# A fixed order on three engines and a ring of five 128x1024 split buffers in an expert stage, with a scatter that leaves out rows without a token

## The chip, the cores and the metric

The kernel runs on one core of a Trainium2 chip. The metric is device time in microseconds (us) for one execution, as the median of several runs. A core has five engines that run side by side and meet through semaphores: PE multiplies matrices (PEld is its weight load), DVE (vector) and ACT (scalar) work elementwise, POOL here mostly issues indirect DMAs, and SP issues plain DMAs. Sixteen DMA engines move the data.

## The reference

The function is one encoder layer: a token mixer (attention and pooling), then a mixture of 32 experts. Only the second half is touched by the change. Each of 1024 tokens goes to two of 32 experts, 2048 places in all, or 64 on average for each expert.

```python
def run_block(args):
    xs, e = args
    gate, up = jnp.split(xs @ w_gate_up[e], 2, axis=-1)
    return (jax.nn.silu(gate) * up) @ w_down[e]
...
out = jax.ops.segment_sum(yb.astype(jnp.float32) * row_w[:, None], row_tok, num_segments=T + 1)
```

An expert multiplies its tokens (rows of 1024 numbers) by a 1024x1024 matrix, whose two halves are gate and up, and the product of silu(gate) and up (512 numbers) by a 512x1024 matrix. The result, weighted, is added to the token's row. Then follows a layer norm over the rows.

## The kernel before, in words

The stages before the experts (projections, attention, output projection, first layer norm, routing) end at about 935 us. The last of them writes the normed rows to `X1` and their scaled copies to `Y` in HBM, and finds for each expert up to 96 rows (`CAP`) of tokens and weights in `first`. What more than 96 tokens an expert has is done in a loop at the end (`overflow`), whose count `count()` works out.

**Precision.** Every product is made of three: a number is split into a high part of reduced width and the remainder (`split`: ACT casts the high part, DVE subtracts to get the low one), and `mm3` adds high x high, high x low and low x high (L165, L166, L167).

**One expert.** `gather` (POOL) fetches its 96 rows into `xg`, four experts ahead. PE transposes them (`X <- xg`, eight 128x96 pieces in two PSUM tiles), and `split` turns these into `xT`, high and low; there is one `xT` buffer. `gu_half` makes `g` with 24 matmuls and `u` with another 24. `hidden` makes `h` from them (`silu` on ACT, the product with `u` on DVE). PE transposes `h` (`X <- h`, four pieces), `split` makes `hT`, and `down` makes two halves `dn` with 12 matmuls each, which ACT weights into `y`. A scatter on POOL then adds `y` to the rows of `Y`. The code is skewed: `down` of expert e-1 is written after the two products of expert e.

**Weights.** An expert has six pieces of 1 MiB (`we`, 128x2048, c = 0 to 5), in a ring of 18 buffers: 15 of the pool `S` and three of the tag `M`. SP issues a load when the buffer's old piece has been split. `weights_` splits a quarter of a piece (128x512, one k of four) into one of five buffers `wh` just before three matmuls use it.

**Order.** Within each engine the scheduler of the framework orders the instructions by its own costs; the set `MOE_ENG` of engines whose order is that of the code is empty. SP's loads keep the order of the program.

**Rows without a token.** An expert's list has 96 entries; those without a token point to row 1024 or above: for the gather past its bound, so that nothing is moved for them, for the scatter to spare rows behind the 1024 real rows of `Y` (96 for each of four groups of experts, cleared by a load of `zero` during attention), so that all 96 rows are added somewhere.

Of the kernel before, what the change touches and what calls it, by code (L numbers as in the profile page):

```python
# [44 lines left out]
NM = 3  # L45
M_AT = (13, 16, 17)
PRE = 5
MOE_ENG = ()
# [5 lines left out]
COUNT_AT = 1  # L54
# [47 lines left out]
def table():  # L102

    t = np.zeros((NE, NBLK, CAP, 4), np.float32)
    t[..., 0] = 4 * T
    t[..., 1] = T + np.arange(NE)[:, None, None] // 8 * CAP + np.arange(CAP)
    return t.reshape(NE * ROWS, 4)


def body(tc, ctx, A, out):  # L110
# [77 lines left out]
    Y = dr.tile([T + 4 * CAP, D], F32, name="Y")  # L188
# [325 lines left out]
    q = SP.dma_start(Y[T:], A["zero"])  # L514
    tc.keep_in_program_order(q)
# [6 lines left out]
    spare = cp.tile([128, 4, 8], F32, name="spare")[:CAP]  # L522
    POOL.iota(spare, pattern=[[CAP, 4], [0, 8]], base=T + 1, channel_multiplier=1, allow_small_or_imprecise_dtypes=True)
# [490 lines left out]
    idx = rt([3, NE], "idx", I32, 1)  # L1014
    tok, wgt = first[:, 0], first[:, 1]

    def rows_at(c, pad):

        no = rt([NE], "no", F32, 3)
        if isinstance(pad, bass.AP) and pad.shape[1] == NE:  # L1020
            DVE.scalar_tensor_tensor(no, tok, 0.0, pad, op0=OP.is_equal, op1=OP.mult)
        else:
            DVE.tensor_scalar(no, tok, 0.0, pad, op0=OP.is_equal, op1=OP.mult)
        DVE.scalar_tensor_tensor(idx[:, c], tok, -1.0, no, op0=OP.add, op1=OP.add)


    rows_at(2, pay[:CAP, 0, 0, 3:4])
# [5 lines left out]
    def transposed(src, n, name, t=None):  # L1033

        t = t or turn_to(n, name)
        for g in range(0, n, 4):
            p = pt([4, CAP], "X", 3)
            for k in range(4):
                PE.transpose(p[:, k], src[:, (g + k) * 128:(g + k) * 128 + 128], ident[:CAP, :CAP])  # L1039
            split(t[:, 0, g:g + 4], t[:, 1, g:g + 4], p)  # L1040
        return t
# [17 lines left out]
    split_ = {}  # L1059

    def weights_(e, c, g):

        if (e, c, g) in split_:
            return split_[e, c, g]
        ahead(stream.index((e, c)) + 1)
        h = split_[e, c, g] = mt([2, 512], "wh", F32R, WH_BUFS)
        split(h[:, 0], h[:, 1], pieces[e, c][:, g])
        return h

    def product(ps, x, e, c, k0):  # L1070

        for g in range(4):
            h, k = weights_(e, c, g), k0 + g
            mm3(ps, (x[:, 0, k], x[:, 1, k]), (h[:, 0], h[:, 1]), k == 0, k == (3 if c >= 4 else 7))
# [306 lines left out]
```

## Time and profile before

| | us |
|---|---|
| median of three runs | 1589.37 (1589.34 to 1590.09) |
| the profiled execution's own time | 1583.73 |
| its span, first to last instruction | 1581.9 |
| experts' stage: first gu matmul to the start of the last dn matmul | 945.80 to 1535.71 |
| granted TensorE clock over the span | 0.978 |

The profile is of one execution, which was 5.6 us shorter than the median of the runs. An engine's busy time in it is the union of its instructions; a matmul's shown length (0.39) holds its way through the array, and the next one starts 0.23 after it.

### The profile page before, as it was taken

What the parts mean: (1) busy time and instruction counts of PE and PEld (TensorE: products, weight loads), DVE (VectorE), ACT (ScalarE), POOL (GpSimd) and SP (SyncE); (2) the same over time, 40 slices, a digit from 0 to 9 for tenths busy, and PEclk for the clock granted to TensorE, in tenths of its full rate; (3) what the DMA queues carried; (4) which work ended last, traced back from release to release, by engine and by line L of the source; (5) the groups of instructions that cost most, each with busy time, mean ns of one, the idle gap of its engine ahead of it and who ended that gap; (6) DMA issues with size and microseconds to landing.
All of it is one profiled execution on the core that took longest, in us unless ns stands there. A gap on an engine that the chain in (4) does not pass through costs nothing.

```text
span 1581.9 us, 23148 instructions
## 1 busy us (share of the span) xinstructions
PE 1504.2 (95%) x7627; PEld 1188.8 (75%) x7627; DVE 1219.3 (77%) x2670; ACT 989.0 (63%) x1955; POOL 336.4 (21%) x232
## 2 busy tenths in 40 slices
PE   8999999999999999999999969999999999999970
PEld 6988888898898898888887856666666666666640
DVE  5774125988988986675567779899999899999867
ACT  4423124676676676674331128888888888888874
POOL 0001000210211210100004440344444444440010
PEclk9999999999999999999999969999999999999995
DMA  7156224855755864427475588999999999999725
GB/s 234 62 175 197 73 80 134 231 191 164 220 190 139 242 193 138 121 97 281 186 283 196 178 290 302 371 381 384 382 385 373 375 380 382 384 380 374 252 31 213
DMA packets 117034, 381.29 MB, mean 241 GB/s; under 512 B 12759, under 2 KB 43863, under 8 KB 91520
## 3 DMA queue, kind: packets, MB, share of 16 engines
q1 hardware_dynamic: 76176, 304.83, 51.5%
q0 software_dynamic: 40160, 74.14, 18.2%
q8 instruction: 61, 1.00, 0.3%
q10 hardware_dynamic: 576, 0.83, 0.2%
q14 instruction: 61, 0.50, 0.1%
HBM read 314.01 MB, written 71.35 MB: 244 GB/s over the span
## 4 chain that ended last, share of the span: by engine, by line
PE 84%; issue 7%; DVE 5%; DMA 2%; ACT 1%; POOL 1%; DVEq 0%; POOLq 0%; SPq 0%; ACTq 0%
PE gu L167 6%; PE gu L166 6%; PE gu L165 6%; PE ps L577 4%; PE pg L165 4%; PE pg L166 4%; PE pg L167 4%; PE po L628 3%; PE dn L166 3%; PE dn L167 3%; PE dn L165 3%; PE X L1039 2%; PE pv L165 2%; PE tp L613 2%; PE pv L167 2%
## 5 line engine op out<-in xcount | busy, mean ns | idle before, releaser
L151 DVE TENSOR_TENSOR wh<-we,wh 128x512 fp32r<-128x512 f32 x768 | 473.0, 683 | 13.6 <-ACT wh L150 10.4
L150 ACT CAST wh<-we 128x512 fp32r<-128x512 f32 x768 | 433.9, 621 | 24.8 <-PE gu L167 6.5
L1083 POOL DMA_INDIRECT xg<-X,idx x32 | 159.9, 4998 | 277.1 <-PE X L1039 266.9
L167 PE MATMUL gu<-wh,xT 128*96 128x512 f32 x512 | 202.8, 396 | 0.0
L165 PE MATMUL gu<-wh,xT 128*96 128x512 f32 x512 | 202.2, 395 | 0.5 <-ACT xT L150 0.5
L166 PE MATMUL gu<-wh,xT 128*96 128x512 f32 x512 | 202.1, 395 | 0.0
L151 DVE TENSOR_TENSOR w<-wraw,w 128x512 fp32r<-128x512 f32 x111 | 75.8, 687 | 92.6 <-ACT w L150 92.2
L150 ACT CAST w<-wraw 128x512 fp32r<-128x512 f32 x111 | 68.5, 621 | 117.7 <-PE pg L167 38.5
L580 ACT ACTIVATE P<-ps,stat 128x256 f32<-128x256 f32 (+7 forms) x128 | 94.8, 741 | 54.7 <-DVE stat L579 53.8
L166 PEld LDWEIGHTS gu<-wh,xT 128*96 128x96 f32 x512 | 83.1, 162 | 36.4
L165 PEld LDWEIGHTS gu<-wh,xT 128*96 128x96 f32 x512 | 83.0, 162 | 36.1 <-ACT xT L150 0.5
L167 PEld LDWEIGHTS gu<-wh,xT 128*96 128x96 f32 x512 | 83.0, 162 | 36.0 <-DVE xT L151 0.5
L166 PE MATMUL dn<-wh,hT 128*96 128x512 f32 x256 | 103.3, 404 | 1.6 <-DVE wh L151 1.5
L165 PE MATMUL dn<-wh,hT 128*96 128x512 f32 x256 | 100.8, 394 | 1.7 <-ACT wh L150 1.7
L167 PE MATMUL dn<-wh,hT 128*96 128x512 f32 x256 | 100.8, 394 | 0.0
L165 PE MATMUL pg<-xT,w 128*128 128x512 f32 x256 | 100.5, 392 | 0.0
L166 PE MATMUL pg<-xT,w 128*128 128x512 f32 x256 | 99.9, 390 | 0.0
L167 PE MATMUL pg<-xT,w 128*128 128x512 f32 x256 | 99.8, 390 | 0.0
L577 PE MATMUL ps<-K,Q 128*128 128x512 f32 (+2 forms) x384 | 98.8, 364 | 0.8 <-DVE z L464 0.8
L579 DVE TENSOR_REDUCE stat<-ps 128x1 f32<-128x256 f32 (+7 forms) x128 | 95.6, 748 | 1.1
L165 PE MATMUL pv<-w,xT 128*128 128x256 f32 x256 | 72.8, 284 | 0.0
L577 PEld LDWEIGHTS ps<-K,Q 128*128 128x128 f32 x384 | 64.7, 189 | 10.7 <-DVE z L464 1.3
(279 smaller groups left out, 3397.3 us busy)
## 6 DMA issues: line engine op xcount, KB each, us to landing
we<-in_we_dram SPq DMA_DIRECT2D x192, 1024.0 KB, 13.6
wraw<-in_w_dram SPq DMA_DIRECT2D x61, 512.0 KB, 3.8
Q<-RQ POOLq DMA_DIRECT2D x64, 256.0 KB, 5.1
RQ<-rh SPq DMA_DIRECT2D x32, 256.0 KB, 3.4
K<-RK POOLq DMA_DIRECT2D x16, 512.0 KB, 4.2
V<-RV POOLq DMA_DIRECT2D x16, 512.0 KB, 5.7
OT<-ohl SPq DMA_DIRECT2D x48, 128.0 KB, 2.3
oT<-OT POOLq DMA_DIRECT2D x6, 1024.0 KB, 10.5
```

Source lines behind the costliest of these rows:

```text
L150: ACT.copy(hi, src)
L151: DVE.tensor_sub(lo, src, r(hi))
L165: PE.matmul(ps, a[0], b[0], start=start, stop=False)
L166: PE.matmul(ps, a[0], b[1], start=False, stop=False)
L167: PE.matmul(ps, a[1], b[0], start=False, stop=stop)
L577: PE.matmul(ps[:, c:c + n], q[:, o, m, qc], Kt[h, m][:, c:c + n], start=o == 0, stop=o == 1)
L579: DVE.tensor_reduce(st_[:, m:m + 1], ps[:, :W], AX.X, OP.max, negate=True)
L580: ACT.activation(Pt[h, i][m][:, :W], ps[:, :W], AF.Exp, bias=st_[:, m:m + 1], accum_out=st_[:, 2 + m:3 + m])
L613: PE.transpose(ps[:, k], p[:, (4 * g + k) * 128:(4 * g + k) * 128 + 128], ident)
L628: PE.matmul(o[:, 0, c], Vt[h][:, a, kt], aT[kt // 4][:, kt % 4, b, c], start=j == 0, stop=j == len(parts) - 1)
L1039: PE.transpose(p[:, k], src[:, (g + k) * 128:(g + k) * 128 + 128], ident[:CAP, :CAP])
L1083: q = POOL.indirect_dma_start(out=x, out_offset=None, in_=X1, in_offset=IO(ap=idx[:, 2 * (e < NXG), expert[e]:expert[e] + 1], axis=0), bou ...
```

## The change

It has three parts.

1. **A fixed order.** PE, ACT and DVE run the experts' stage in the order of the code (`manual_schedule`), and the code is rewritten for that. `product` counts the halves of pieces that PE has used (`state["used"]`); after each one it issues the split of the half that is five ahead (`split_next`), and then whatever was put there to be done (`put(n, ...)`: after n more halves). So the transposes of `h` stand after `g`, those of `xg` after `u`, and the casts, `silu`, the product `h*u`, the weighting `y` and the scatter stand one to three halves behind the matmuls that they need.
2. **Wider splits.** A split is of 128x1024 (two k, six matmuls), in a ring of five such buffers. The ring of pieces is 16 instead of 18 (`NM` 1 for 3).
3. **No spare rows.** The scatter's index of an entry without a token lies past its bound and is left out, as the gather's is; the spare rows, their clearing, and the index list for them are gone. The overflow loop's buffers come from the pool `S`.

```diff
-NM = 3
-M_AT = (13, 16, 17)
-PRE = 5
-MOE_ENG = ()
+NM = 1
+M_AT = (13,)
...
-    Y = dr.tile([T + 4 * CAP, D], F32, name="Y")
+    Y = dr.tile([T, D], F32, name="Y")
...
-    q = SP.dma_start(Y[T:], A["zero"])
...
+    parts = [(e, c, g) for e, c in stream for g in range(2)]
...
+    def split_next():
+        if state["split"] < len(parts):
+            e, c, g = parts[state["split"]]
+            state["split"] += 1
+            ahead(stream.index((e, c)) + 1)
+            h = mt([2, 2, 512], "wh", F32R, WH_BUFS)
+            split(h[:, 0], h[:, 1], pieces[e, c][:, 2 * g:2 * g + 2])
+            ring.append(h)
...
+    def product(ps, x, c, k0):
+
+        for g in range(2):
+            h = ring.popleft()
+            for i in range(2):
+                k = k0 + 2 * g + i
+                mm3(ps, (x[:, 0, k], x[:, 1, k]), (h[:, 0, i], h[:, 1, i]), k == 0, k == (3 if c >= 4 else 7))
+            state["used"] += 1
+            split_next()
+            for f in todo.pop(state["used"], ()):
+                f()
...
-                                    bounds_check=T + 4 * CAP - 1, oob_is_err=True, compute_op=OP.add)
...
+                                    bounds_check=T - 1, oob_is_err=False, compute_op=OP.add)
...
+    with tc.manual_schedule(engines={mybir.EngineType.PE, mybir.EngineType.Activation, mybir.EngineType.DVE}):
...
+        for _ in range(WH_BUFS):
+            split_next()
+        for g, p in enumerate(transposes(gx.pop(0), 8)):
+            taken(x, g, p)
...
+            g = gu_half(x, 0)
+            if e:
+                hT = turn_to(4, "hT")
+                put(1, taken, hT, 0, transposes(h, 4)[0])
+            put(2, ACT.activation, h, g, AF.Silu)
+            u = gu_half(x, 2)
             if e + 1 < NE:
-                x = transposed(gx.pop(e + 1), 8, "xT")
+                x = turn_to(8, "xT")
+                for i, p in enumerate(transposes(gx.pop(e + 1), 8)):
+                    if e:
+                        put(1 + i, taken, x, i, p)
+                    else:
+                        taken(x, i, p)
+            put(3 if 0 < e < NE - 1 else 1, DVE.tensor_mul, h, h, u)
             if e:
                 down(e - 1, hT)
+        hT = turn_to(4, "hT")
+        taken(hT, 0, transposes(h, 4)[0])
+        down(NE - 1, hT)
```

Three places show what this does to the order. On PE, in the middle of the experts' stage, this is where `down` of one expert begins, with the transposes of `h` and of the next `xg` (`X`):

```order
L165 MATMUL dn_11066<-wh_11075,hT_10987 96x512
L1039 MATMUL X_11182<-cst,h_9634 128x96 x4
L1039 MATMUL X_11245<-cst,xg_9574 128x96 x4
L1039 MATMUL X_11252<-cst,xg_9574 128x96 x4
L166 MATMUL dn_11066<-wh_11075,hT_10987 96x512
L167 MATMUL dn_11066<-wh_11075,hT_10987 96x512
```

Before, all twelve transposes stand in one block, after the fourth matmul of `dn`, between the first and the second of three matmuls of one k. With the change the four of `h` stand between `g` and `u`, five halves of pieces later than the product that makes `h`:

```order
L164 MATMUL gu_10707<-wh_10688,xT_10644 96x512
L1029 MATMUL X_10753<-cst,h_9630 128x96 x4
L162 MATMUL gu_10758<-wh_10701,xT_10644 96x512
L163 MATMUL gu_10758<-wh_10701,xT_10644 96x512
L164 MATMUL gu_10758<-wh_10701,xT_10644 96x512
```

The eight of `xg` stand behind `u`, ahead of `dn`. On DVE, at the same place, these rows before are the product `h` and what stands around it:

```order
L151 TENSOR_TENSOR wh_10681<-we_10679,wh_10681 128x512
L1096 TENSOR_TENSOR h_9634<-h_9634,gu_10607 96x512
L151 TENSOR_TENSOR xT_10662<-X_10663,xT_10662 128x384
L151 TENSOR_TENSOR xT_10662<-X_10670,xT_10662 128x384
L151 TENSOR_TENSOR wh_10687<-we_10679,wh_10687 128x512
L151 TENSOR_TENSOR wh_10693<-we_10679,wh_10693 128x512
```

And these with the change:

```order
L148 TENSOR_TENSOR wh_10347<-we_10323,wh_10347 128x1024
L148 TENSOR_TENSOR xT_10328<-X_10329,xT_10328 128x384
L148 TENSOR_TENSOR wh_10360<-we_10358,wh_10360 128x1024
L148 TENSOR_TENSOR xT_10328<-X_10334,xT_10328 128x384
L148 TENSOR_TENSOR wh_10372<-we_10358,wh_10372 128x1024
L1080 TENSOR_TENSOR h_9630<-h_9630,gu_10284 96x512
```

The three jobs that stood together now stand one behind each split. On PE at the stage's start, before, the first expert's eight transposes and four of the second expert's stand ahead of the first product:

```order
L1039 MATMUL X_9660<-cst,xg_9573 128x96 x4
L1039 MATMUL X_9667<-cst,xg_9573 128x96 x4
L1039 MATMUL X_9763<-cst,xg_9574 128x96 x4
L165 MATMUL gu_9677<-wh_9645,xT_9633 96x512
L166 MATMUL gu_9677<-wh_9645,xT_9633 96x512
```

With the change only the first expert's eight do:

```order
L898 MATMUL pr_9453<-ohr_9534 96x64 x2
L1029 MATMUL X_9652<-cst,xg_9570 128x96 x4
L1029 MATMUL X_9657<-cst,xg_9570 128x96 x4
L162 MATMUL gu_9669<-wh_9637,xT_9629 96x512
L163 MATMUL gu_9669<-wh_9637,xT_9629 96x512
```

The second expert's transposes of `xg` all stand behind the first expert's `u`.

## Rows read from the trace of the kernel before

**Rows 1.** The page: the span and the engines' busy time.
```profile
span 1581.9 us, 23148 instructions
PE 1504.2 (95%) x7627; PEld 1188.8 (75%) x7627; DVE 1219.3 (77%) x2670; ACT 989.0 (63%) x1955; POOL 336.4 (21%) x232
```

**Rows 2.** A stretch: length; busy PE, PEld, DVE, ACT, POOL; clock, DMA share, GB/s.
```profile
1000.00:1100.00 100.00, 100.00 (x458) 69.03 (x457) 91.26 (x152) 88.42 (x163) 40.04 (x11) 1.00 1.02 377
```

**Rows 3.** Instructions in order of time, one expert's transposes: start, us, what [idle before].
```profile
1100.21 0.86 ACT L150 CAST xT<-X 128x384 fp32r<-128x384 f32 x2 [1.47 <-PE gu L167]
...
1100.82 1.01 DVE L151 TENSOR_TENSOR xT<-X,xT 128x384 fp32r<-128x384 f32 x2
...
1100.95 0.55 PE L1039 MATMUL X<-cst,h 96*128 96x96 f32 x4
...
1101.47 1.03 PE L1039 MATMUL X<-cst,xg 96*128 96x96 f32 x8
1101.75 1.88 DVE L151 TENSOR_TENSOR wh<-we,wh 128x512 fp32r<-128x512 f32 x3
1102.48 0.16 PEld L166 LDWEIGHTS dn<-wh,hT 128*96 128x96 f32 x1 [0.17 <-DVE wh L151]
...
1102.79 0.40 PE L167 MATMUL dn<-wh,hT 128*96 128x512 f32 x1
```

**Rows 4.** PE in order of time: six transposes of an early expert.
```profile
974.63 0.49 PE L1039 MATMUL X<-cst,h 96*128 96x96 f32 x4
974.96 0.33 PE L1039 MATMUL X<-cst,xg 96*128 96x96 f32 x2
...
975.36 0.39 PE L167 MATMUL dn<-wh,hT 128*96 128x512 f32 x1
```

**Rows 5.** PE: first gu matmuls of experts 3, 9, 31; first dn matmul behind 9's.
```profile
997.35 0.39 PE L165 MATMUL gu<-wh,xT 128*96 128x512 f32 x1
...
1107.19 0.39 PE L165 MATMUL gu<-wh,xT 128*96 128x512 f32 x1
...
1118.31 0.39 PE L165 MATMUL dn<-wh,hT 128*96 128x512 f32 x1
...
1509.98 0.39 PE L165 MATMUL gu<-wh,xT 128*96 128x512 f32 x1
```

**Rows 6.** Splits by shape: count, busy us, mean ns of one, idle time before them.
```profile
L151 DVE TENSOR_TENSOR wh<-we,wh 128x512 fp32r<-128x512 f32 x763 | 469.7, 683 | 12.6 <-ACT wh L150 9.4 <-DMA we<-in_we_dram 1.7
L150 ACT CAST wh<-we 128x512 fp32r<-128x512 f32 x763 | 431.1, 621 | 20.9 <-PE gu L167 6.5 <-PE dn L167 2.6
...
L151 DVE TENSOR_TENSOR xT<-xr,xT 128x1024 fp32r<-128x1024 f32 x8 | 9.8, 1225 | 6.2 <-ACT xT L150 6.2
L150 ACT CAST xT<-xr 128x1024 fp32r<-128x1024 f32 x8 | 8.4, 1051 | 12.0 <-DMA xr<-in_xT_dram 12.0
```

**Rows 7.** PE at the stage's start, in order of time, and the clock there.
```profile
940.81 1.54 PE L1039 MATMUL X<-cst,xg 96*128 96x96 f32 x8 [5.99 <-DMA xg<-X,idx]
945.19 0.90 PE L1039 MATMUL X<-cst,xg 96*128 96x96 f32 x4 [2.84 <-DMA xg<-X,idx]
945.80 0.72 PE L165 MATMUL gu<-wh,xT 128*96 128x512 f32 x1
...
959.67 0.47 PE L165 MATMUL gu<-wh,xT 128*96 128x512 f32 x1 [0.46 <-ACT xT L150]
...
945.80:949.30 3.50, 3.50 (x10) 2.31 (x10) 0.69 (x1) 1.22 (x2) 1.90 (x2) 0.50 0.84 167
```

**Rows 8.** PE at the stage's end, in order of time.
```profile
1529.19 0.47 PE L165 MATMUL dn<-wh,hT 128*96 128x512 f32 x1 [1.66 <-ACT wh L150]
...
1535.71 0.39 PE L167 MATMUL dn<-wh,hT 128*96 128x512 f32 x1
```

**Rows 9.** Loads of weights in 1000 to 1100 and 1360 to 1460: us to landing.
```profile
we<-in_we_dram SPq DMA_DIRECT2D x33, 1024.0 KB, 11.9
...
we<-in_we_dram SPq DMA_DIRECT2D x34, 1024.0 KB, 17.1
```

More of the change, by code (lines that the diff above doesn't have):

```diff
@@ L1019, in rows_at @@
         no = rt([NE], "no", F32, 3)
[L1020 to L1023, printed above, removed]
+        DVE.tensor_scalar(no, tok, 0.0, pad, op0=OP.is_equal, op1=OP.mult)
         DVE.scalar_tensor_tensor(idx[:, c], tok, -1.0, no, op0=OP.add, op1=OP.add)
-    rows_at(2, pay[:CAP, 0, 0, 3:4])
+    rows_at(1, pay[:CAP, 0, 0, 3:4])
     xgs = [rt([D], f"xg{i}", F32, 1) for i in range(NXG)]
@@ L1057, in ahead, with put @@
             pieces[e, c] = w
[L1059 to L1074, printed above, removed]
+    parts = [(e, c, g) for e, c in stream for g in range(2)]
+    ring = deque()
+    todo = {}
+    def split_next():
[6 more added lines that the diff above has]
+            ring.append(h)
+    def put(n, f, *a):
+        todo.setdefault(state["used"] + n, []).append(partial(f, *a))
+    def product(ps, x, c, k0):
[8 more added lines that the diff above has]
+                f()
     ahead(13)
@@ L1086, in gather, with gu_half, scatter, weighted @@
         return x
-    def gu_half(e, x, c):
+    def gu_half(x, c):
         ps = pt([512], "gu", 3, CAP)
-        product(ps, x, e, c, 0)
-        product(ps, x, e, c + 1, 4)
-        return ps
-    def hidden(h, g, u):
-        ACT.activation(h, g, AF.Silu)
-        DVE.tensor_mul(h, h, u)
-        return h
+        product(ps, x, c, 0)
+        product(ps, x, c + 1, 4)
+        return ps
+    def scatter(e, y):
+        q = POOL.indirect_dma_start(out=Y, out_offset=IO(ap=idx[:, 0, expert[e]:expert[e] + 1], axis=0), in_=y, in_offset=None,
+                                    bounds_check=T - 1, oob_is_err=False, compute_op=OP.add)
+        for i, o in enumerate(ysc):
+            if i % 4 != e % 4:
+                tc.declare_no_dep(q.ins, o.ins, reason="another group's rows of Y")
+        ysc.append(q)
+    def weighted(e, y, n, d):
+        ACT.activation(y[:, n * 512:n * 512 + 512], d, AF.Copy, scale=wgt[:, expert[e]:expert[e] + 1])
+        if n:
+            scatter(e, y)
     def down(e, hT):
@@ L1102, in down @@
             d = pt([512], "dn", 2, CAP)
-            product(d, hT, e, 4 + n, 0)
-            ACT.activation(y[:, n * 512:n * 512 + 512], d, AF.Copy, scale=wgt[:, expert[e]:expert[e] + 1])
-        q = POOL.indirect_dma_start(out=Y, out_offset=IO(ap=idx[:, 1, expert[e]:expert[e] + 1], axis=0), in_=y, in_offset=None,
-                                    bounds_check=T + 4 * CAP - 1, oob_is_err=True, compute_op=OP.add)
-        for i, o in enumerate(ysc):
-            if i % 4 != e % 4:
-                tc.declare_no_dep(q.ins, o.ins, reason="another group's rows of Y")
-        ysc.append(q)
+            product(d, hT, 4 + n, 0)
+            put(1, weighted, e, y, n, d)
     def count():
-        pc = pt([2 + 2 * NE + 1], "X", 3)
+        pc = pt([512], "gu", 3)[:, :2 + 2 * NE + 1]
+        ov, ovi = mt([NE], "ov", F32, 1)[:1], mt([2 * NE + 1], "ovi", I32, 1)[:1]
         v, b = mt([3], "cv", F32, 1)[:NE], mt([2 * NE + 1], "cb", BF, 1)[:NE]
@@ L1133, in count @@
         DVE.tensor_scalar(ovi[:, NE:2 * NE], ov, 1.0, float(CAP), op0=OP.add, op1=OP.mult)
-        return ovi
+        yield ovi
     def overflow(x, ovi):
```

62 lines of the change are left out of this document (29 added, 33 removed).

## The prediction

> **What bounds the kernel now.** I read the page first: PE is busy for 95% of the span [rows 1], so a change pays only where PE waits, works slowly, or has nothing to do. The view by stretches then shows the experts' stage: 100 us of PE in 100 us at the full clock, DVE at 91%, ACT at 88%, and a DMA share of 1.02 [rows 2]. That reads as if nothing were left for PE, and it misleads: a matmul's shown length includes its way through the array, so short waits vanish inside it. They show in the starts.
>
> The starts give the period of an expert: from expert 3 to expert 31 [rows 5] it is (1509.98 - 997.35) / 28 = 18.31 us. The work in it is 72 matmuls and 12 transposes. A run of 48 matmuls without a break takes 1118.31 - 1107.19 = 11.12 us [rows 5], 0.2317 each, so 72 cost 16.68. The remaining 1.63 go with the transposes. In time order [rows 3], the block runs from 1100.95 to the next free matmul at 1102.79, 1.84 us, which holds one matmul: 1.60 for twelve transposes. In an early expert, where nothing made them wait, six took 975.36 - 974.63 - 0.23 = 0.50 [rows 4], 0.083 each, so twelve cost 0.99. The difference, 0.6 us for each expert, is waiting.
>
> Rows 3 also tell for what. The two PSUM tiles for `xg` are still full: `xT` has one buffer, so its casts start when `u` is done (ACT 1.47 us idle before them), DVE ends its two at 1101.83, and the eight transposes of `xg` take 1101.47 to 1102.48, 1.01 instead of 0.66. Behind them, `dn` waits for a split that queued behind those casts. So the bound is PE, stretched by DVE jobs that come in a clump. The loads are not waited for.
>
> **The change part by part.**
>
> *The transposes.* With the order printed above, `h` is transposed five halves of pieces after the product that makes it, and the tiles for `xg` are emptied one and two halves after they are filled, most of an expert before their next use. A half is six matmuls, 1.39 us. So every wait of rows 3 should go. The period becomes 16.68 + 0.99 = 17.67; I take 17.7 for some change-over. The gain is 0.6 for each of 28 experts, 17.0 us. Bounds: 0, if waits of the same size come back elsewhere, and 1.63 - 0.99 = 0.64, 17.9 us.
>
> *The wide splits.* 128x1024 costs 1.051 on ACT and 1.225 on DVE, against 0.621 and 0.683 for half of it [rows 6]. For an expert, 12 replace 24: DVE loses 16.4 - 14.7 = 1.7 us by shown lengths, ACT 14.9 - 12.6 = 2.3. Shown lengths overlap a little, so the lower bound is nothing. Even then DVE's 0.91 of 18.31 is 16.7 us [rows 2], under 17.7: it stays second. The price is latency: a half is ready 1.05 + 1.23, with passing about 2.5 us, after PE lets the buffer go. PE needs it four halves later, 5.6 us. Between stand at most a `y`, `xT` or `h` job for each half, about 0.5 to 0.7 us each [rows 3, 6], and PE's pace leaves DVE 0.25 us a half to catch up, so it is never more than about 1 us behind. Some 2 us of cover remain; without it PE would wait up to twelve times for each expert.
>
> *The loads.* Two buffers fewer mean that a load is issued 16 pieces ahead instead of 18. A piece lasts 17.7 / 6 = 2.95 us, so 16 give 47 us. Landing takes 11.9 us early in the stage and 17.1 near its end [rows 9]. This creep is the one sign that DMA is close to its limit: 5.2 us over 360 us, or 0.26 for each expert, so the loads now run at a pace of 18.57. The scatter's part shrinks: 96 - 64 = 32 rows of 4 KB for an expert, 0.13 MB of 6.29 (weights) + 0.26 (gather) + 0.39 (scatter) = 6.94. At 6.94 / 18.57 = 374 GB/s, 6.81 MB take 18.2 us. PE at 17.7 gains 0.5 on that for each expert, 15 us over 29: landing ends at some 27 us, under 47. Cost nothing.
>
> The stretch moved 377 GB/s in all [rows 2]. The Trainium skill, "DMA: Bandwidth & Descriptors", Specifications, gives about 358 GB/s of HBM for each core, which would speak against a faster PE. By that, 6.81 MB would take 19.0 us an expert, landing would reach 50 us at the end and PE would lose some 3 us, so the sum would be 3 us worse; rows 2 show that this core alone gets more, and I go by them.
>
> *The start.* Now four transposes of the second expert's `xg` stand ahead of the first product, and PE waits 2.84 us for that gather [rows 7]. With the change the product starts when the first `xT` is split, about 942.5 instead of 945.80. But the clock is at 0.50, and eight matmuls take 3.5 us until 949.3 [rows 7]. If the clock rises at the same moment, sixteen are slow and of 3.3 us only 1.7 remain; if it rises 3.3 earlier, all does. Slow ones cost 3.5 / 8 - 0.23 = 0.2 more each, so the first expert ends at 942.5 + 11.1 + 3.3 = 956.9, or at 955.2. Then a loss: the second `xT` is not made ahead. Its first split follows the last wide one (ACT 1.05 + 0.45, DVE another 1.23 + 0.5), 3.2 us that hold the transposes' 0.66. So the second expert starts at 960.1 or 958.4, against 959.67 [rows 7]; I take 959.3. The next two experts take 2 x 17.7 and about 0.55 for the three small products of `count`, to 995.25, against 997.35 [rows 5]. Gain 2.1, bounds 0 and 4.
>
> *The end.* From expert 31's first matmul to the last now takes 1535.71 - 1509.98 = 25.73, with a wait of 1.66 for a late split [rows 5, 8]. With the change the splits run out four halves before the end and are early; 95 matmuls are 22.01, eight transposes 0.66, and the last `hT` has nothing to hide it: a cast on each engine, near 0.45 and 0.5 by the `xT` casts [rows 3], and passing, 1.0. That is 23.7, a gain of 2.0, bounds 1 and 3.
>
> *The rest at nothing.* The clearing load and the index list lie beside attention, where PE is the bound; PE's order there shifts slightly in the first heads, which I take as 0, within 0.7. The overflow loop's body does not run. A shorter last scatter may save some tenths.
>
> **Sum.** 17.0 + 2.1 + 2.0 = 21.1 us. The profiled span of 1581.9 would become 1560.8, and its own time 1583.7 would become 1562.6. The median of the runs is 5.6 us above that execution, outside what these terms touch, so I take the gain off it: 1589.4 - 21.1 = 1568.3 us.
>
> **The rivals.**
>
> *Half of the waits return.* The fixed order could make PE wait at another place: the split of `xT` after `u` has the least cover, about 1 us on DVE. For it speaks that each engine now works strictly in turn and cannot step round a late job; against it, the cover computed above. With 0.3 us for each expert: 8.5 less, 1576.8.
>
> *It does not do what it says.* If all 0.6 us come back, only start and end remain, 4.1 us: 1585.3. The DMA share of 1.02 speaks for it, the 47 us of ring against it.
>
> *Loads run dry (slower).* Place: PE's first matmul of a half, behind a split, behind a load. Landing must pass 47 us within 29 experts: (47 - 12) / 29 = 1.2 above 17.7, a pace of 18.9, or 360 GB/s. The kernel gets slower than before only when the 21 us are lost too: 19.6 us, 347 GB/s. At 340 GB/s an expert takes 20.0, and 29 x 0.4 more gives 1601. The creep speaks for it; the 377 GB/s against it [rows 2].
>
> By the page's figure named above this rival would begin to cost, but not reach the point where it makes the kernel slower.
>
> *More than forecast.* Clock early, shorter scatter, no change-over: 24 us, 1565.
>
> **How the numbers follow.** Chances: forecast 0.70, half of the waits 0.17, nothing in the middle 0.04, loads dry 0.03, more 0.06. The forecast's own range is 1566 to 1573. To leave no more than 2 in 10 outside, the range takes in the second case and the edge of "more": 1564.5 to 1578. A difference of 0.2%, 3.2 us, is about what can be told from none. All cases but the loads are faster by more, the middle one only just, so I halve it: faster 0.95, same 0.02, slower 0.03.
>
> **What would show it.** The first matmuls of successive experts 17.7 us apart; transposes 0.083 apart in their groups, with no idle before them put to DVE; DVE near 0.85 of a stretch; the first product at about 942.5 and the last near 1514.6; landing growing beyond 20 us with no PE wait put to `we`. Wrong would be a period over 18.0, and then the releaser of PE's weight load says which cover failed; or PE waiting for `xT` early in each expert. The first product at 942.5 with expert 1 later than 960.1 would make the start wrong.

## The result, and the profile after

The changed kernel takes 1568.09 us (median of four runs, 1567.38 to 1568.57), the kernel before in the same session 1589.73 (1589.34 to 1590.52): a ratio of 0.9863, 95% interval 0.9846 to 0.988. The forecast was 1568.3, with a range of 1564.5 to 1578. One execution of the kernel before, in the session of the first experiments, took 3048.8 us and is left out of every range here.

That is close by more than one accident, and the profiles say so. The two profiled executions take 1583.73 and 1567.72 us: 16.0 less, where the sum was 21.1. The steady part and the end came as worked out. The way to the stage and its start were 5.6 us worse than forecast. And the forecast was taken from a median that lies 5.6 us above the profiled execution of the kernel before, while the changed kernel's median lies 0.4 above its own. That two differences of this size met is luck.

The page of the changed kernel gives the span, the engines' busy time and the loads (median us to landing):

```profile
span 1565.9 us, 22004 instructions
...
PE 1489.4 (95%) x7627; PEld 1190.3 (76%) x7627; DVE 1195.5 (76%) x2284; ACT 945.7 (60%) x1571; POOL 270.0 (17%) x231
...
we<-in_we_dram SPq DMA_DIRECT2D x192, 1024.0 KB, 21.7
```

PE in order of time, from the first transposes of the stage to its last matmul:

```profile
945.30 1.54 PE L1029 MATMUL X<-cst,xg 96*128 96x96 f32 x8 [6.46 <-DMA xg<-X,idx]
946.78 0.74 PE L162 MATMUL gu<-wh,xT 128*96 128x512 f32 x1
...
959.42 0.82 PE L1029 MATMUL X<-cst,xg 96*128 96x96 f32 x8
962.11 0.47 PE L162 MATMUL gu<-wh,xT 128*96 128x512 f32 x1 [1.86 <-ACT xT L147]
...
963.65 0.74 PE L164 MATMUL gu<-wh,xT 128*96 128x512 f32 x1 [0.84 <-DVE xT L148]
...
976.71 0.82 PE L1029 MATMUL X<-cst,xg 96*128 96x96 f32 x8
977.32 0.45 PE L162 MATMUL dn<-wh,hT 128*96 128x512 f32 x1
...
1000.87 0.39 PE L162 MATMUL gu<-wh,xT 128*96 128x512 f32 x1
...
1112.48 0.49 PE L1029 MATMUL X<-cst,h 96*128 96x96 f32 x4
1112.75 0.45 PE L162 MATMUL gu<-wh,xT 128*96 128x512 f32 x1
...
1495.73 0.39 PE L162 MATMUL gu<-wh,xT 128*96 128x512 f32 x1
...
1519.39 0.39 PE L164 MATMUL dn<-wh,hT 128*96 128x512 f32 x1
```

The starts give the period: expert 3 at 1000.87, expert 31 at 1495.73, (1495.73 - 1000.87) / 28 = 17.67 us, against 18.31 [rows 5]. The twelve transposes stand where the order puts them, and nothing makes them wait: eight move the next matmul by 0.61 us, four by 0.27. From expert 31's first matmul to the last is 23.66 us. What went wrong shows higher up: the first product starts at 946.78, later than before [rows 7], expert 1 at 962.11 after waits of 1.86 and 0.84 us, and expert 3 stands 3.5 us behind its place in the kernel before [rows 5].

The view by stretches (length; busy PE, PEld, DVE, ACT, POOL; clock, DMA share, GB/s), for one stretch of the stage and three short ones in which the clock is low:

```profile
1000.00:1100.00 100.00, 100.00 (x474) 71.14 (x473) 91.27 (x92) 84.99 (x103) 24.99 (x11) 1.00 1.01 375
...
851.00:854.40 3.40, 3.40 (x11) 2.82 (x11) 2.74 (x17) 0.39 (x2) 0.50 (x1) 0.50 0.82 269
...
946.78:949.95 3.17, 3.17 (x9) 2.08 (x9) 1.09 (x2) 0.74 (x2) 2.56 (x3) 0.50 1.05 306
...
963.65:967.05 3.40, 3.40 (x8) 2.00 (x9) 0.67 (x2) 1.04 (x1) 0.00 (x0) 0.50 0.99 310
```

DVE's share is 0.91 of a shorter period, 16.1 us an expert for 16.7 before [rows 2]: busy, and still behind PE. At 851.0 the clock falls to its lower level, 1.2 GHz, for 3.4 us, where the kernel before keeps 2.4 GHz; at 963.65 it falls again, after PE has waited twice for the second expert's `xT`.

### The profile page after: what moved, and what is told of

Its sections match the earlier page's. It is cut to its first block, busy times and chain, and to the rows that moved or that the text cites. A ratio compares the mean times of both kernels' runs of the same rounds, so it can differ in the third digit from the quotient of the medians.

```text
span 1565.9 us, 22004 instructions
## 1 busy us (share of the span) xinstructions
PE 1489.4 (95%) x7627; PEld 1190.3 (76%) x7627; DVE 1195.5 (76%) x2284; ACT 945.7 (60%) x1571; POOL 270.0 (17%) x231
## 4 chain that ended last, share of the span: by engine, by line
PE 54%; issue 29%; POOL 9%; DVE 5%; ACT 2%; DMA 2%; POOLq 0%; DVEq 0%; SPq 0%; ACTq 0%
POOL Y L1101 7%; PE ps L570 4%; PE pg L162 4%; PE pg L163 4%; PE pg L164 4%; PE po L621 3%; POOL xg L1089 2%; PE pa L162 2%; PE pa L164 2%; PE pa L163 2%; PE pv L162 2%; PE pv L164 2%; PE tp L606 2%; PE pv L163 2%; PE pw L162 2%
## 5 line engine op out<-in xcount | busy, mean ns | idle before, releaser
L148 DVE TENSOR_TENSOR wh<-we,wh 128x1024 fp32r<-128x1024 f32 x384 | 460.4, 1219 | 57.3 <-ACT wh L147 53.3
L147 ACT CAST wh<-we 128x1024 fp32r<-128x1024 f32 x384 | 401.4, 1046 | 93.4 <-PE gu L164 61.8
L1101 POOL DMA_INDIRECT Y<-y,idx x32 | 104.6, 3268 | 271.8 <-ACT y L1109 267.0
```

Of the source, the lines that this page charges most:

```text
L147: ACT.copy(hi, src)
L148: DVE.tensor_sub(lo, src, r(hi))
L1101: q = POOL.indirect_dma_start(out=Y, out_offset=IO(ap=idx[:, 0, expert[e]:expert[e] + 1], axis=0), in_=y, in_offset=None, bounds_check=T - ...
```

## The experiments

Each ran in three or five rounds beside the kernel before. This table has what the traces say of each; the period is that from expert 3 to expert 31, all times in us.

| kernel | median (range of runs) | first product | expert 3 | expert 31 | period | last matmul |
|---|---|---|---|---|---|---|
| before | 1589.73 (1589.34 to 1590.52) | 945.80 | 997.35 | 1509.98 | 18.31 | 1535.71 |
| changed | 1568.09 (1567.38 to 1568.57) | 946.78 | 1000.87 | 1495.73 | 17.67 | 1519.39 |
| b_same | 1586.90 (1583.79 to 1592.35) | 946.71 | 997.79 | 1510.41 | 18.31 | 1536.15 |
| b_xt2 | 1605.96 (1604.10 to 1606.93) | 948.67 | 999.83 | 1527.96 | 18.86 | 1554.61 |
| b_code | 1832.04 (1823.70 to 1838.69) | 945.18 | 1016.35 | 1760.14 | 26.56 | 1789.76 |
| b_wide | 1596.94 (1594.47 to 1598.26) | 950.18 | 1001.55 | 1522.06 | 18.59 | 1550.20 |
| a_narrow | 1575.05 (1572.51 to 1578.34) | 956.81 | 1011.20 | 1506.05 | 17.67 | 1529.64 |
| a_spare | 1572.49 (1569.21 to 1574.74) | 950.08 | 1004.04 | 1498.90 | 17.67 | 1522.57 |
| a_wh4 | 1572.16 (1571.32 to 1573.76) | 950.02 | 1005.00 | 1499.85 | 17.67 | 1524.97 |
| a_wh3 | 1584.16 (1581.39 to 1587.00) | 948.10 | 1002.90 | 1508.15 | 18.04 | 1535.07 |
| a_now | 1570.36 (1567.71 to 1573.00) | 950.79 | 1005.62 | 1500.47 | 17.67 | 1524.28 |
| a_start | 1568.08 (1563.26 to 1568.25) | 950.73 | 1001.44 | 1496.85 | 17.69 | 1520.52 |
| a_pre | 1565.47 (1563.79 to 1566.17) | 944.82 | 999.64 | 1494.77 | 17.68 | 1518.44 |
| a_best | 1560.95 (1559.50 to 1563.17) | 944.47 | 994.92 | 1489.78 | 17.67 | 1513.46 |

Between the changed kernel and those whose edits lie behind the first product, that product moves by several microseconds. So the medians mix two things, the way to the stage and the stage itself, and the columns keep them apart.

**b_same: the kernel before, unchanged.**

> The kernel before, unchanged, to find the 5.6 us between its profiled execution (own time 1583.7 us) and its timed runs (1589.4). Theory: own time is span + 1.8 in every execution, so the spans will be near 1587.5, and a profile of such an execution shows the 5.6 us at one place ahead of the experts' steady part or at the stage's start, while the period of an expert stays 18.31 us. Rival: the period itself differs from execution to execution (18.31 in one, 18.5 in another: 0.19 x 28 = 5.3), and then the gain in the steady part was larger than the two profiles show.

Ten runs gave 1583.79 to 1592.35, and the kernel before, run beside it, 1584.14 to 1590.20. The profile is again that of a quick execution (span 1581.9), with the same period, 18.31. Own time is span + 1.8 in each of these ten runs, within 0.1. The granted clock of the span goes with the time: 0.978 at a span of 1581.9, 0.975 at 1588.0, 0.974 at 1590.6. So the 5.6 us lie within the kernel's own spread, and the longer runs have a lower mean clock. Where the time lies in a longer execution no trace shows, since none of one was taken: that part of the theory stays open, and so does the rival, a period that varies.

**b_xt2: a second `xT` buffer for the old order.**

```diff
-XT_BUFS = 1
+XT_BUFS = 2
-NM = 3
-M_AT = (13, 16, 17)
+NM = 2
+M_AT = (13, 16)
```

> The kernel before with two buffers for xT (and a ring of 17 pieces for 18, to make room). Theory: the eight transposes of xg wait because the casts into the one xT buffer start only when u is done; with two, the tiles are emptied early and most of the 0.6 us for each expert goes: period 17.7 to 18.0, time 1573 to 1581. Rival: the waits come from the order in which the scheduler puts the jobs, whatever the buffers: period 18.2 to 18.4, time 1586 to 1591. Second rival, loads at the limit: the period cannot fall, and landing creeps up.

The time went the other way, and both rivals were too mild: the period rose to 18.86, ratio 1.0125 (1.0106 to 1.0143). But where the theory looked, among the transposes of [rows 3], it held. First the kernel before, at the two places where a full tile is met:

```profile
1101.26 0.25 PE L1039 MATMUL X<-cst,h 96*128 96x96 f32 x1
1101.47 0.27 PE L1039 MATMUL X<-cst,xg 96*128 96x96 f32 x1
...
1101.74 0.25 PE L1039 MATMUL X<-cst,xg 96*128 96x96 f32 x1
1101.98 0.27 PE L1039 MATMUL X<-cst,xg 96*128 96x96 f32 x1
```

From the last transpose of `h` to the first of `xg` it is 0.21 us, and from the fourth of `xg` to the fifth 0.24, where 0.08 is the step without a wait. Each time PE goes on 0.1 to 0.15 us after a subtraction of `xT` on DVE has emptied the tile (the two of [rows 3] end at 1101.37 and 1101.83), and the step behind it is longer by 0.03 as well. That is 0.33 us for each expert. With two `xT` buffers both waits are gone; the four of `h` take 0.39 us to the first of `xg` instead of 0.52:

```profile
1220.84 0.55 PE L1039 MATMUL X<-cst,h 96*128 96x96 f32 x4
1221.23 0.41 PE L1039 MATMUL X<-cst,xg 96*128 96x96 f32 x3
```

The rest of the 0.6 us lies at the two ends of the block. Step by step against the changed kernel, as means over experts 3 to 31: 0.08 around the first two transposes of `h`, which come up on PE just before the product `h` is made, and 0.22 at `dn`, for the late split. Together with the tiles' 0.33 that is 0.63, the difference of the two periods.

The view of waits alone would have misled. Its columns are what waited, for what, us in all, times, longest, here from 1000 to 1100, five experts; on PE such short waits show in its weight loads. The kernel before:

```profile
PEld X L1039 <- DVE h L1096: 1.6, 5, 0.3
PEld dn L166 <- DVE wh L151: 0.9, 5, 0.2
```

The two waits for tiles are missing, since on the weight load each is under 0.15 us, the least that this view lists. And 0.3 us of an idle weight load before `h` hold back PE's matmuls by 0.08 only. With two `xT` buffers:

```profile
PEld gu L166 <- DVE wh L151: 7.6, 15, 0.9
PEld X L1039 <- DVE h L1096: 1.6, 5, 0.3
```

The wait for `h` is untouched. The casts of `xT` have moved into the next expert's `g`, where they stand with those of `hT` ahead of the splits on DVE, and PE now waits there three times for each expert, which costs more than the tiles' waits did:

```profile
1209.96 0.55 DVE L151 TENSOR_TENSOR hT<-X,hT 128x384 fp32r<-128x384 f32 x1
1210.43 0.55 DVE L151 TENSOR_TENSOR xT<-X,xT 128x384 fp32r<-128x384 f32 x1
1210.89 2.48 DVE L151 TENSOR_TENSOR wh<-we,wh 128x512 fp32r<-128x512 f32 x4
```

A buffer was freed, the scheduler used it, and the clump went to a place with less cover.

**b_code: the old code's own order, held fixed.**

```diff
-MOE_ENG = ()
+MOE_ENG = ("PE", "Activation", "DVE")
```

> The kernel before with PE, ACT and DVE held to the order of its own code (nothing else changed). Theory: it is not a fixed order as such that brings the gain but where the jobs stand in it. In the old code the splits of dn stand behind the casts of xT on ACT, and those of u behind the casts of hT, so at both places PE waits for a transpose, a cast, a subtraction, a split: about 0.5 + 0.5 + 0.6 + 0.7 and passing, 2 to 2.5 us each, 3 to 4.5 for each expert: 1680 to 1730 us. Rival: the order alone takes the clumps away: period 17.7, about 1570.

Right in direction and far too small: 1832 us, ratio 1.153 (1.1495 to 1.1565), a period of 26.56. ACT in order of time, one expert:

```profile
1048.43 0.48 ACT L150 CAST hT<-X 128x384 fp32r<-128x384 f32 x1 [3.07 <-PE X L1039]
1048.80 4.27 ACT L150 CAST wh<-we 128x512 fp32r<-128x512 f32 x8
...
1056.14 0.86 ACT L150 CAST xT<-X 128x384 fp32r<-128x384 f32 x2 [2.58 <-PE X L1039]
...
1061.15 0.68 ACT L1104 ACTIVATE y<-dn,first 96x512 f32<-96x512 f32 x1 [2.07 <-PE dn L167]
...
1065.96 0.68 ACT L1104 ACTIVATE y<-dn,first 96x512 f32<-96x512 f32 x1 [2.06 <-PE dn L167]
```

Four times for each expert ACT waits for the end of a product with the next splits queued behind it, 3.07 + 2.58 + 2.07 + 2.06 = 9.8 us; then PE waits for those splits, 22.1 us in all from 1000 to 1100, under four experts. The expectation counted two such places and missed the two `y`. The waits also cost clock: between expert 3 and expert 31 the clock is at 0.50 in 19 stretches, 68 us together, which hold back up to 34 us of work, 1.2 for each expert; the expectation had no term for that. A fixed order has no value of its own: what the change adds is the places of the jobs in it, the splits five halves ahead of their use above all.

**b_wide: the wide splits without the order.** Splits of 128x1024 in five such buffers and 16 pieces in the ring, as in the change; the order is the scheduler's.

```diff
-        h = split_[e, c, g] = mt([2, 512], "wh", F32R, WH_BUFS)
-        split(h[:, 0], h[:, 1], pieces[e, c][:, g])
+        h = split_[e, c, g] = mt([2, 2, 512], "wh", F32R, WH_BUFS)
+        split(h[:, 0], h[:, 1], pieces[e, c][:, 2 * g:2 * g + 2])
...
-            h, k = weights_(e, c, g), k0 + g
+            h, k = weights_(e, c, g // 2), k0 + g
```

> The kernel before with splits of 128x1024 in a ring of five such buffers, its ring of pieces 16 for 18, and the scheduler's order as before. Theory: the wide split brings nothing of itself, since DVE is not the bound; the waits at the transposes stay, and a job of 1.2 us in the clump makes them no shorter: period 18.2 to 18.6, time 1587 to 1600. Rival: the gain comes from fewer and cheaper splits: period near 17.7, time 1572.

As the theory had it: 18.59, ratio 1.0061 (1.0043 to 1.0079). The same view of waits, 1000 to 1100:

```profile
PEld gu L166 <- DVE wh L151: 6.0, 11, 0.8
PEld dn L166 <- DVE wh L151: 1.6, 9, 0.2
```

The buffers are as many and as large as in the changed kernel, and PE waits for splits all the same, since the scheduler's order does not fill them ahead: counted in the traces at the start of each expert from 3 to 31, one wide split is done ahead of PE here, and three in the changed kernel.

**a_narrow: the order without the wide splits.** Each wide buffer is filled by two narrow splits.

```diff
-            split(h[:, 0], h[:, 1], pieces[e, c][:, 2 * g:2 * g + 2])
+            for i in range(2):
+                split(h[:, 0, i], h[:, 1, i], pieces[e, c][:, 2 * g + i])
```

> The changed kernel with its order and its ring kept, but each 128x1024 buffer filled by two splits of 128x512. Theory (the gain is the order's, not the width's; DVE stays second): DVE's shown work for an expert goes from 16.1 us (0.913 of 17.67) to that of before, 16.7, still under 17.67, and a half is ready no later: period 17.67 to 17.75, time 1568 to 1571. Rival: with 16.7 of 17.67 DVE has too little room for the y, xT and h jobs between, and PE waits for splits: period 18.0 or more, 1577 and up.

The period is that of the changed kernel, 17.67. The median is 7 us longer, outside the theory's range; in the profiled execution the first product came 10 us later, at 956.81, of which 6.9 are a first gather that took 11.6 us. a_spare, with wide splits, had the same slow gather, so the narrow splits need not be its cause. From the view by stretches:

```profile
1000.00:1100.00 100.00, 100.00 (x477) 71.12 (x476) 94.30 (x159) 89.19 (x170) 39.05 (x12) 1.00 1.02 371
```

DVE is busy for 0.943 of 17.67, 16.7 us as in the kernel before, and PE waits for nothing. The wide split spares DVE 0.6 us for each expert, and the period does not need them.

**a_spare: the rows without a token scattered again.** The index list, the load that clears the spare rows, their 384 rows of `Y` and the old bound are back; order and rings are the changed kernel's.

> The changed kernel with the spare rows back: all 96 rows of an expert are scattered, the load that clears them and the index list are back. Theory: 0.13 MB more for each expert, 6.94 MB in 17.67 us is 393 GB/s; at some 375 the loads lose 0.8 us for each expert, landing goes from 12 to some 36 us at the end, under the 47 us of the ring, so the period stays 17.67 and the time is within 2 us of the changed kernel's 1568.1. Rival: DMA is at its limit and the skipped rows are what lets the order pay: period 17.9 to 18.5, 1575 to 1590. Aside: if the 2.5 us that the changed kernel loses at the beginning of attention come from the clearing load or the index list that were taken out, the stage begins 2 to 3 us earlier here.

The period is 17.67, and loads land after 24.0 us in 1360 to 1460, against 24.4 in the changed kernel: the rows that are left out save nothing that PE waits for. Two stretches:

```profile
250.00:300.00 50.00, 49.16 (x258) 41.32 (x257) 41.30 (x97) 32.39 (x74) 10.05 (x15) 1.00 0.68 201
1360.00:1460.00 100.00, 100.00 (x479) 71.31 (x478) 90.98 (x90) 84.02 (x102) 24.01 (x10) 1.00 1.02 380
```

The stage moved 380 GB/s, so the 358 of the Trainium skill, "DMA: Bandwidth & Descriptors", Specifications, by which the prediction worked out 50 us of landing, do not bind here. The Trainium skill, "Perfetto Trace Analysis", Roofline, says that 358 is a core's share when both cores of a pair use the memory, and that one alone can get more, up to some 435; the 380 agree with that.

The aside came true for the way to the stage, though the slow gather hides it in the first product. PE is busy for 49.16 of 250 to 300, as in the kernel before, and for 47.52 in the changed one; routing's last product (`pr`) stands at 934.9, against 938.5 in the changed kernel. What does it is neither the load nor the use of the list: a_pre puts back the iota alone that makes the list, and its trace has the order of this run on PE up to the stage; without the iota, the scheduler orders the first heads of attention differently. The median is 4.4 us above the changed kernel's, where the theory allowed 2; in the profiled execution the first gather took 11.6 us here, for 4.7 there.

**a_wh4 and a_wh3: four and three wide buffers.**

```diff
-WH_BUFS = 5
+WH_BUFS = 4
```

> The changed kernel with four wide buffers instead of five. A half is then split when PE has used the one four ahead of it, and needed three halves later, 4.2 us. Theory (ready 2.5 us after the buffer is let go, 2 us of cover with five): 0.6 us of cover are left, less than one y, xT or h job, so PE waits a little at the places where two stand together: period 17.7 to 18.1, 1569 to 1581. Rival, the cover was never needed: exactly 17.67. Second rival, the cover was overrated and DVE's queue is the limit: over 18.3, slower than the kernel before.

> The changed kernel with three wide buffers instead of five. A half is needed two halves after PE lets its buffer go, 2.8 us, and in the changed kernel's trace it is ready 0.34 + 1.05 + 1.23 = 2.6 us after. Theory: 0.2 us of cover, less than any y, xT or h job in between (0.5 to 0.7 us), of which DVE has four and ACT six for each expert, so PE waits at several halves: period 18.3 to 20, time 1587 to 1640. Rival (with four buffers PE waited nowhere, so the queues have more slack than was worked out): period under 18, below 1578.

Four buffers give 17.67, with no wait in the steady part: the first rival. What the fifth changes shows at the end, where the time from expert 31 to the last matmul is 25.12 us instead of 23.66. Three give 18.04, which is between theory and rival, ratio 0.9979 (0.9966 to 0.9992). There PE waits for DVE (1000 to 1100):

```profile
PEld gu L163 <- DVE wh L148: 5.0, 12, 0.6
```

These 5.0 us are idle time of the weight load; PE's period loses 0.37 for each expert. Most of that is lost at one place, in `g`, behind a split that follows the product `h` on DVE (`h` from 1022.39, the split done at 1024.20, PE's next matmul at 1024.26). So the cover was worked out too small; why the other jobs cost nothing is not shown.

**a_now: the jobs between the splits bunched again.** PE's order is that of the changed kernel, row for row, and so are the splits; the other jobs of ACT and DVE follow their product at once.

```diff
-                put(1, taken, hT, 0, transposes(h, 4)[0])
-            put(2, ACT.activation, h, g, AF.Silu)
+                taken(hT, 0, transposes(h, 4)[0])
+            ACT.activation(h, g, AF.Silu)
             u = gu_half(x, 2)
+            DVE.tensor_mul(h, h, u)
...
-                    if e:
-                        put(1 + i, taken, x, i, p)
-                    else:
-                        taken(x, i, p)
-            put(3 if 0 < e < NE - 1 else 1, DVE.tensor_mul, h, h, u)
+                    taken(x, i, p)
...
-            put(1, weighted, e, y, n, d)
+            weighted(e, y, n, d)
```

> The changed kernel with PE's order and the splits five halves ahead kept, but every other job of ACT and DVE put right behind the product that it follows, instead of one to three halves later. On DVE the product h and the two subtractions of xT then stand together behind one split, 0.68 + 1.1 + 1.23, as clumped as in the kernel before. Theory A (PE's order and the look-ahead carry the gain): a half is ready 2.6 us after its buffer is let go and needed after 5.6, the clump adds 1.8, so PE waits nowhere and the period stays 17.67 to 17.75, 1567 to 1572. Theory B, that of the prediction's account of the kernel before (it is the clump on DVE that stretches PE): period 17.9 to 18.3, 1574 to 1587.

Theory A: the period is 17.67 with this on DVE, the clump of [rows 3]:

```profile
1212.76 1.23 DVE L148 TENSOR_TENSOR wh<-we,wh 128x1024 fp32r<-128x1024 f32 x1 [0.16 <-ACT wh L147]
1213.90 0.68 DVE L1222 TENSOR_TENSOR h<-h,gu 96x512 f32<-96x512 f32 x1
1214.50 1.01 DVE L148 TENSOR_TENSOR xT<-X,xT 128x384 fp32r<-128x384 f32 x2
```

So a clump on DVE is not enough to stretch PE. It did in the kernel before, where the transposes of `xg` met tiles that the clump was just emptying, and `dn` a split that stood behind it. Spacing these jobs out is worth nothing once PE's order and the splits' lead are those of the change.

**a_start: the second expert's `xT` earlier.**

```diff
             state["used"] += 1
-            split_next()
+            if state["used"] != 8:
+                split_next()
...
         for _ in range(WH_BUFS):
             split_next()
+        warm = mt([1], "warmS", F32, 1)
+        ACT.activation(warm, eps, AF.Silu)
...
                         taken(x, i, p)
+                if not e:
+                    split_next()
```

> The changed kernel with two edits at the stage's start: a small Silu on ACT right after the first five splits, so that its table is loaded while ACT waits for the first gather, and the split behind the first expert's last half put behind the casts of the second xT. Theory: in the changed kernel's trace PE waits 1.86 us at 962.11 and 0.84 us at 963.65, and the clock falls to 0.50 from 963.65 to 967.07, because the table load (1.28 us), silu and a wide split stand ahead of the xT casts on ACT. Without them expert 2 starts 3 to 4.5 us earlier, and the time is 1564 to 1565.5. Rival: the wait moves to the late split (PE waits for it in the second expert's first halves) or the clock falls all the same: 1567 to 1568.5.

The two kernels' ACT at the end of the first expert, first the changed kernel, then this one:

```profile
956.84 1.05 ACT L147 CAST wh<-we 128x1024 fp32r<-128x1024 f32 x1 [0.34 <-PE gu L164]
957.91 1.28 ACT L1080 ACT_TABLE_LOAD   x1
959.21 0.59 ACT L1080 ACTIVATE h<-gu 96x512 f32<-96x512 f32 x1
959.70 1.98 ACT L147 CAST wh<-we 128x1024 fp32r<-128x1024 f32 x2
961.58 0.85 ACT L147 CAST xT<-X 128x384 fp32r<-128x384 f32 x2
```

```profile
962.32 0.59 ACT L1081 ACTIVATE h<-gu 96x512 f32<-96x512 f32 x1
962.81 1.04 ACT L147 CAST wh<-we 128x1024 fp32r<-128x1024 f32 x1
964.48 0.86 ACT L147 CAST xT<-X 128x384 fp32r<-128x384 f32 x2 [0.64 <-PE X L1029]
```

The casts now wait for PE instead of PE for them. The changed kernel takes 54.09 us from the first product to expert 3, this one 50.71: 3.4 less, as the theory had it. No low stretch follows the second expert's start, and from expert 1 to 3 it takes 36.43 instead of 38.77. The median, 1568.08, did not move and lies where the rival had it, though not by the rival's cause: the profiled execution, 1568.25, reached its first product 3.95 us later than the changed kernel's, and 3.5 of these lie ahead of both edits, before the last `pr`. For the three runs without a trace that is not shown. The gain shows in this trace and in a_best.

The Trainium skill, "ScalarE: Activation LUTs", What ACT_TABLE_LOAD costs, gives 1283 ns for the load and about 1380 for a drain with it. The trace has the 1.28 us; no drain shows beside it (the split before ends at 957.89, silu starts at 959.21).

**a_pre: the iota back, and one split ahead of the first `xT`.** The iota stands as it did before, and nothing reads it.

```diff
+    POOL.iota(spare, pattern=[[CAP, 4], [0, 8]], base=T + 1, channel_multiplier=1, allow_small_or_imprecise_dtypes=True)
...
-        for _ in range(WH_BUFS):
-            split_next()
+        split_next()
         for g, p in enumerate(transposes(gx.pop(0), 8)):
             taken(x, g, p)
+        for _ in range(WH_BUFS - 1):
+            split_next()
```

> The changed kernel with two edits ahead of its first product: the index list's iota on POOL is back (nothing reads it; with it the scheduler puts PE's attention in the order of the kernel with the spare rows), and only one of the first five wide splits stands ahead of the casts of the first xT, the other four behind them. Theory: the iota gives the 2.3 to 4.9 us back that PE's attention lost, and the last small product of routing (pr) stands near 935 instead of 938.5; with one split, no piece is free before the first gather has landed, so no 1 MiB load is issued beside it, and it lands within 5 us of its issue (11.6 us in two of the profiles so far), the first product at about 943, expert 3 at about 997, the time 1564 to 1565, and the runs lie closer together than those of the kernel before (1584 to 1593). Rival: the gather is slow for another reason (its own descriptors, the stores of the normed rows); then landing stays between 4 and 12 us and the runs spread over 1564 to 1571.

Half of it came: attention is back in step (the last `pv` product starts at 577.8, in the changed kernel at 580.0, before at 577.6), but a low stretch of the clock from 860.7 to 864.1 took some of it again, and the last `pr` stands at 937.1 instead of 935. The gather landed in 4.2 us, here and 5.2 in a_best. The first product is 2.0 us earlier than in the changed kernel, the ratio to before 0.9857 (0.9842 to 0.9873). Whether the loads were what held up the gather is not settled. In the seven profiles of the changed kernel and its relatives in which a load is issued 1.5 to 2.2 us behind the gather, it took 4.4 to 5.2 us five times and 11.6 twice, so two short ones here prove little. In all five profiles whose first load comes 2.7 us behind the gather or later (before, b_same, b_code, a_pre, a_best) it took 4.1 to 5.2; in b_xt2 and b_wide, with a load 1.6 to 1.7 us behind, 8.3 and 8.0. That speaks for the loads without showing it.

**a_best: a_pre and a_start together.**

> The edits of a_pre and a_start together, with nothing else changed. Theory: they act at different places, so their gains add: first product at about 943, expert 3 some 51 us later at 994, last matmul at 1512 to 1513, time 1560 to 1562, below the kernel before and the changed one. Rival: the split postponed behind the second xT now meets an emptier ring, and PE waits for it: 1563 to 1566.

Theory: 1560.95 us (1559.5 to 1563.17), ratio to before 0.9834 (0.982 to 0.9848), for 0.9863 (0.9846 to 0.988) of the changed kernel: the intervals just touch, and the trace shows where the time went. PE in order of time:

```profile
944.47 0.74 PE L162 MATMUL gu<-wh,xT 128*96 128x512 f32 x1
...
994.92 0.39 PE L162 MATMUL gu<-wh,xT 128*96 128x512 f32 x1
...
1513.46 0.40 PE L164 MATMUL dn<-wh,hT 128*96 128x512 f32 x1
```

From the first product to expert 3 it takes 50.45 us, and the last matmul stands 5.9 us ahead of the changed kernel's.

## Why the prediction was right, and where it was not

*The steady part: right in size, and right in cause but for the clump.* 17.67 was worked out as 16.68 for 72 matmuls and 0.99 for twelve transposes that wait for nothing, and 17.67 it is; the gain is (18.31 - 17.67) x 28 = 17.8 us, for 17.0 with a margin. That the 0.6 us were waiting at the transposes, for full `xg` tiles with the one `xT` buffer behind them and for a late split, was right: the trace has 0.33 for the tiles and 0.22 for the split. The 0.35 that the prediction read off the tiles (1.01 us instead of 0.66) holds both, and the 0.08 for `h` it did not see. That a clump on DVE by itself stretches PE was wrong (a_now). Nor is it enough to free the tiles: a second `xT` buffer takes away the tiles' wait and makes the period longer (b_xt2). What carries the gain is the place of the transposes on PE, those of `h` late and those of `xg` into tiles that have long been empty, together with splits that run far ahead. No run moves one of the two groups of transposes alone, so their shares are read from the steps in the trace and not tested one by one. Order and depth are each needed: the depth without the order gives 18.59 (b_wide), the order with three buffers 18.04 (a_wh3), with four or five 17.67, a fixed order without the look-ahead 26.56 (b_code).

*The wide splits: right that they cost nothing,* and it turned out that they bring nothing to the period either (a_narrow). DVE "near 0.85 of a stretch" was wrong: 0.91, since the shown work fell by 0.6 us for each expert, not by 1.7. Two microseconds of cover was an underestimate; PE begins to wait only when three buffers are left of five.

*The loads: right.* Landing is 24.4 us late in the stage, "some 27" at the end was the forecast, 47 the limit, and no wait of PE is put to a load. The rival that turns the kernel slower did not come near: with 0.13 MB more for each expert the period did not change (a_spare). The skipped scatter rows are worth nothing here.

*The end: right.* 23.66 us for 23.7. The stretch from the last matmul to the end of the span stayed (46.2 before, 46.5 after), so the shorter last scatter saved nothing.

*The start and "the rest at nothing": these steps failed.* The forecast for expert 3 was 995.25, the trace has 1000.87. The 5.6 us, step by step:

- "PE's order there shifts slightly in the first heads, which I take as 0, within 0.7": the last `pr` is at 938.48 instead of 934.46, 4.0 us. Of these 2.4 are there by the last `pv` in attention, which the scheduler ordered differently once the iota was gone (a_spare, a_pre); some 1.7 is the low clock at 851.0 to 854.4, which no step had.
- The first gather lands 0.5 us later behind `pr`, and the product follows its transposes 0.2 sooner than worked out.
- The first expert takes 15.33 us, 1.5 less than the 16.8 in the sum: the clock rose 3.2 us after the product's start.
- Experts 1 and 2 take 38.77 instead of 35.95, 2.8 more. The step counted 3.2 us from the first expert's end to the first half of the second `xT`, and that part was not too small: 959.42 to 962.11, 2.7. It put nothing for the second half. DVE had two wide splits to do ahead of it, since silu, its table load and two splits stood ahead of the casts on ACT; PE waited for another 0.84 us at 963.65, and then the clock was low for 3.4 us, which costs 1.7. That is 2.5 of the 2.8. a_start takes the table load and the last split away, and 2.3 come back. The sign that the prediction named, expert 1 later than 960.1, does not tell this: the product was 4.3 us late to begin with, and from it to expert 1 the time was shorter than forecast.

4.0 + 0.5 - 0.2 - 1.5 + 2.8 = 5.6.

*The base.* The sum was taken off 1589.4, the median of three runs, on the ground that the 5.6 us between it and the profile lay outside the terms. They do, but they are no constant: the kernel before spreads over 1583.0 to 1593.0 in the sessions of this study, with medians of 1587 to 1590. Three runs in the upper half of that and a start that was 5.6 us worse than forecast met at 1568; that the number came so close is luck. From profile to profile the gain is 16.0, and 1589.4 - 16.0 = 1573.4 would lie in the range too.

## What to carry to other kernels

Where matmuls of one pass are never shown to wait, take the period from their starts, and find the wait by the steps from one start to the next, against a place or a kernel where nothing waits. A view of waits leaves out the short ones, and idle time of the weight load is not time that PE loses: here it named half of the cause and missed the other. A fixed order pays by what runs ahead in it, and jobs may stand bunched if the look-ahead covers the bunch; a ring of buffers that the order does not fill ahead was worth nothing here. Freeing one buffer can move a wait to a place where it costs more. And before the end of a chain is costed, list everything that its engine does in the last two steps, table loads too, and check that an edit elsewhere has not changed the order that a scheduler gives to stages far from it.

## What the runs showed of the hardware

A wait can cost more than itself: in the changed kernel PE waits 1.86 and 0.84 us at the second expert's start, the lower clock from 963.65 to 967.05 comes right behind, and 3.4 us at 1.2 GHz hold 1.7 us of work at 2.4 GHz. The seven profiles of the changed kernel and its relatives without a_start's edits all have two waits there, 2.5 to 2.8 us together, and all have such a stretch beside them, beginning between 963.1 (a_pre) and 974.8 (a_narrow); a_start and a_best, with 0.2 and 0.7 us of waiting, have none. A stretch of the same length appears ahead of the stage in the changed kernel at 851.0 and in a_pre at 860.7, and in the kernel before in neither of its two profiles. The mean clock of the span goes with the time of a run of the kernel before (0.978 at 1581.9, 0.974 at 1590.6).

A first gather of 96 rows landed 4.1 to 11.6 us after its issue. In the two long cases its own instruction on POOL takes 5.9 and 6.1 us, in the changed kernel 1.2, so what was held up is its issue, not only its data. POOL at that place, in a_narrow and then in the changed kernel:

```profile
943.71 6.12 POOL L1090 DMA_INDIRECT xg<-X,idx  x1 [8.57 <-ACT wh L147]
```

```profile
940.53 1.23 POOL L1089 DMA_INDIRECT xg<-X,idx  x1 [8.83 <-ACT wh L147]
```

What held it up in one execution and not in the other stays open.
